# Expert results by indirect transfers through a table in DRAM, in place of matmuls with selection matrices

## The chip, the core and the metric

The kernel runs on one core of a Trainium2 chip. The metric is the device time of one execution in microseconds. Five engines work side by side, each through its own queue in order: PE (TensorE, matmul), DVE (VectorE), ACT (ScalarE), POOL (GpSimd) and SP (SyncE, which here only issues transfers). In this kernel SP issues every transfer and POOL none.

## What is computed

A trunk of two layers works on 272 tokens (16 learned ones and 256 of the input) of 1024 channels: a Griffin recurrent block and a dense SwiGLU, then gated linear attention and a mixture of experts. Each of the four sub-layers ends in `LayerNorm(alpha * x + sublayer(x))`. The change touches the last sub-layer only. Its reference, cut to the core:

```python
logits = hf @ router
top_logit, top_idx = lax.top_k(logits, 2)
top_w = softmax(top_logit)
gates = einsum('nk,nke->ne', top_w, one_hot(top_idx, 8))
for e in range(8):
    y = y + gates[:, e:e+1] * ((silu(hf @ w_gate[e]) * (hf @ w_up[e])) @ w_out[e])
```

Each token goes to two of eight experts. Every expert has 1024 x 7168 and 3584 x 1024 weights in float32, 44 MB, and all of them are read once.

## The kernel before

All large matmuls are done in three passes (`mm3`, L271 to L275): weights and activations are each split into a high and a low part, and low by high, high by low and high by high are summed. The activations (128 x 128) are loaded into the array, and 512 columns of weights stream by. The class `Weights` streams all weights of the program in one fixed order. SP loads units of 128 x 2048 (1 MB) into places of SBUF (`load`, L97), as soon as a place is free; ACT writes the high part of each piece of 1024 columns (`whi`, L127) and DVE the low part (`wlo`, L137), four pieces ahead of the matmuls that take them. When the low part of a unit's last piece is written, its place goes to the next unit. A place can be retired, which hands it to another use.

The experts run one after another, each with room for 128 tokens; a branch at the end repeats the work for more, and it isn't taken when no expert has over 128. An expert has seven blocks (`JM`), so there are 56 blocks `n`. A block is `stage_in` (8 steps `k`, each with three matmuls into the gate bank `pg` and three into the up bank `pu`), four transposes of the product (`stage_tr`, tile `pt`, L1273, done in the next block after three steps), and `stage_out` (24 matmuls into the two output banks `y` of the expert). So a block has 72 matmuls of 512 columns and four transposes. DVE does 12 low parts, one product and one split for it.

Tokens are routed by matmul. `select` (DVE, L931) makes a 0/1 matrix from ranks: tokens by slots of an expert.

- Before a pair of experts, `gather` multiplies the 256 token rows, split in high and low (`x3h`, `x3l`), by the pair's matrices (L940: 32 matmuls of 256 columns for a pair, tile `xg`); ACT and DVE apply gain and bias (L1037, L1035), then split the rows (L268, L269, tile `xe`). Experts 0 and 1 get theirs ahead of the expert loop.
- `slots(e)` transposes the expert's matrix (two transposes, tile `st`, L1229) and fetches the gate of each slot (two matmuls, tile `gs`, L1234).
- After an expert, `evacuate` multiplies its result by the gates and splits it (ACT L1304, DVE L1307), and `combine` multiplies it by the transposed matrix (L1314 and L1315: 8 matmuls of 512 columns an expert, tile `cb`), which DVE adds to the rows `acc` in SBUF (L1317).
- For the last expert, `combine` adds into the banks `total`, into which `add_rows` has put `acc`, split by `split_acc`. Then the final norm follows.

This extra work waits in a list (`Side`). At every second step `k` of `stage_in` one item is taken from it, with up to four saved up. `rows_1` fills the list in expert 0 when the place `xeB` comes free: the rows of expert 1 are split, gates computed, and `acc` is multiplied by the norm's gain, alpha, and added to the bias by `residual` (with `pick` on POOL, L1191, and `sp` on PE, L1197). In the loop at the end of the function the remaining items are put in by block. The framework orders each engine's instructions by priority and by when it reckons them ready.

Fifteen places hold weights when the experts start: nine of the program's own, `late0` to `late3`, `xeC` and `xeB`. `xeB` is retired at block 2 and `xeC` at block 6, and 13 are left.

Of the kernel before, what the change touches and what calls it, by code (L numbers as in the profile page):

```python
# [11 lines left out]
F32 = mybir.dt.float32  # L12
F32R = mybir.dt.float32r
# [172 lines left out]
def trunk_kernel(ctx: ExitStack, tc: tile.TileContext, xT_d, rgp_d, lnT_d, rgin_d, rgg_d, rgout_d,  # L186
# [50 lines left out]
    def bank(name):  # L237
        return ps.tile([P, 512], F32, tag="ps", name=name)
# [678 lines left out]
    pos = small("pos", [P, 2, NE])  # L917
    sels = {}
    late = ctx.enter_context(tc.tile_pool(name="late", bufs=1, reuse_waits="tile"))
    W.widen([(late, "late0"), (late, "late1"), (late, "late2"), (late, "late3"), (late, "xeC")])  # L920
    gb = ctx.enter_context(tc.tile_pool(name="rows", bufs=1, reuse_waits="tile"))
    x3T = [gb.tile([P, 2, NX], F32, tag="xg", name=f"x3T{k2}", bufs=4) for k2 in range(4)]

# [101 lines left out]
    xe, xgs = {}, {}  # L1025

    def rows_of(e):
        pool, tag = ((m2, "xeA"), (m2, "xeB"), (late, "xeC"))[e % 3]
        t = pool.tile([P, 2, KD, P], F32R, tag=tag, name=f"xe{e}", bufs=1)
        xe[e] = (t[:, 0], t[:, 1])  # L1030

    def affine(out, pk, kk, vector):
# [6 lines left out]
    def gathered(pg, e0, k2):  # L1039

        if k2 == 0:
            rows_of(e0)
            rows_of(e0 + 1)
        xg = gb.tile([P, 2, 2, P], F32, tag="xg", name=f"xgs{e0}{k2}", bufs=4)
        for k in range(2):
            affine(xg[:, k], pg[:, k * 256:(k + 1) * 256], 2 * k2 + k, k == 1)
        xgs[e0, k2] = xg

    def first_rows(k2, e):

# [109 lines left out]
    w1 = small("w1", [P, 2, 1])  # L1160
    w2 = small("w2", [P, 2, 1])

    def gate_values():
        pn = bank("count")
        nc.tensor.matmul(pn[:, :NE], ones, mask[:, 0], start=True, stop=False)
        nc.tensor.matmul(pn[:, :NE], ones, mask[:, 1], start=False, stop=True)
        nc.vector.tensor_reduce(cnt, pn[:, :NE], axis=mybir.AxisListType.X, op=ALU.max)
        nc.vector.tensor_copy(cnti, cnt)
        nc.vector.tensor_sub(o2, mask, o1)
        nc.vector.tensor_sub(df, top[:, :, 1:2], top[:, :, 0:1])  # L1170
        nc.scalar.activation(df, df, AF.Exp)
        nc.vector.tensor_scalar_add(w1, df, 1.0)
        nc.vector.reciprocal(w1, w1)
        nc.vector.tensor_mul(w2, df, w1)
        nc.vector.tensor_mul(o1, o1, w1.broadcast_to([P, 2, NE]))
        nc.vector.tensor_mul(o2, o2, w2.broadcast_to([P, 2, NE]))
        nc.vector.tensor_add(gates, o1, o2)

    picks, rows_hl = {}, []

# [22 lines left out]
    def residual(c, s, i):  # L1203

        if i == 0:
            spreads[c, s] = spread(0, c, s)
        a = acc[:, i, s * 512:(s + 1) * 512]
        nc.vector.scalar_tensor_tensor(a, spreads[c, s], ALPHA, a, op0=ALU.mult, op1=ALU.add if c else ALU.mult)


    gslot = m2.tile([P, NE], F32, name="gslot")
    selT = {}
    gus, hts, ys, yes = {}, {}, {}, {}

# [4 lines left out]
    def gather(e0, k2):  # L1219
        pg = bank(f"xg{e0}{k2}")  # L1220
        for i in range(2):
            gather_part(pg, k2, e0, i)
        gathered(pg, e0, k2)

    def slots(e):
# [6 lines left out]
        pg = bank(f"gs{e}")  # L1232
        for i in range(2):
            nc.tensor.matmul(pg[:, :NE], sel_of(e)[:, i].bitcast(F32), gates[:, i], start=(i == 0),  # L1234
                             stop=(i == 1), skip_group_check=True)
        nc.vector.tensor_copy(gslot[:, e:e + 1], pg[:, e:e + 1])

    rows = m2.tile([P, 256], F32, name="rows")
    nc.gpsimd.memset(rows, 0.0)
    for n in range(2):  # L1240
        for p0 in (64 * n, 64 * n + 32):
# [3 lines left out]
    def rows_1():  # L1245
        side.put([lambda: rows_of(1)] + [lambda k2=k2: split_rows(1, k2) for k2 in range(4)]
                 + [spread_split, lambda: behind(chosen, gate_values)]
                 + [lambda c=c: spread_pick(0, c) for c in range(2)]
                 + [lambda c=c, s=s, i=i: residual(c, s, i) for c in range(2) for s in range(2) for i in range(2)])

    def stage_in(n):
        e = n // JM
        xeh, xel = xe[e]
        pg, pu = bank(f"pg{n}"), bank(f"pu{n}")
        for k in range(KD):
            if k == 3 and n > 0:
                stage_tr(n - 1)
            for pp in (pg, pu):
                mm3(pp, (xeh[:, k], xel[:, k]), W.take(512), k == 0, k == KD - 1)
            if k % 2:  # L1260
                side.step()
# [21 lines left out]
    def stage_out(n):  # L1283
# [7 lines left out]
        for b, (q, s) in enumerate(blocks):  # L1291
# [6 lines left out]
            if n == NJ - 1 and b == 6:  # L1298
                finish(0)

    def evacuate(e, s):
        g = gslot[:, e:e + 1]
        yh, yl = [gb.tile([P, 512], F32R, tag="xg", name=f"y{t}{e}{s}", bufs=4) for t in "hl"]
        high = nc.scalar.activation(yh, ys[e][s], AF.Copy, scale=g)  # L1304
        if (e, s) == (NE - 1, 0):
            preload_sqrt(high)
        nc.vector.scalar_tensor_tensor(yl, ys[e][s], g, yh, op0=ALU.mult, op1=ALU.subtract)  # L1307
        yes[e, s] = yh, yl

    def combine(e, i, s):  # L1310
        yh, yl = yes[e, s]
        c = slice(s * 512, (s + 1) * 512)
# [77 lines left out]
    for n in range(NJ + 1):  # L1390
        if n == 1:
            W.after = ()
        if n < NJ:
            stage_in(n)
        if n > 0:
            e, j = (n - 1) // JM, (n - 1) % JM
            if n == NJ:
                side.drain()
            stage_out(n - 1)
            if n == RB:  # L1400
                W.retire("xeB", rows_1)
            if n == JM - 1:
                W.retire("xeC", lambda: None)
            if j == (2 if e % 2 else 4):
                side.put([lambda e=e: slots(e)])
            if j == 2 and e % 2 == 1 and e < NE - 1:
                side.put([lambda e=e: pair(e + 1)])
                side.put([lambda g=g: behind(chosen, lambda: [select(g, i) for i in range(2)]) for g in (e + 1, e + 2)])
                side.put([lambda e=e, k2=k2: gather(e + 1, k2) for k2 in range(4)])
                side.put([lambda g=g, k2=k2: split_rows(g, k2) for g in (e + 1, e + 2) for k2 in range(4)])  # L1410
            if e == NE - 1 and j == 1:
                lng[0] = m2.tile([P, 2, D], F32, tag="xeA", name="lng", bufs=1)
                side.put([lambda c=c: spread_pick(1, c) for c in range(2)] + [lambda: None] * 4)
# [3 lines left out]
            if j == JM - 1:  # L1417
                while e not in selT:
                    side.items.popleft()()
                if e < NE - 1:  # L1420
                    evacuate(e, 0)
                    evacuate(e, 1)
                    side.put([lambda e=e, i=i, s=s: combine(e, i, s) for s in range(2) for i in range(2)])
    evacuate(NE - 1, 1)
    finish(1)

# [160 lines left out]
```

## Time and profile before

| what | value |
|---|---|
| runs | 1553.68, 1556.21, 1557.07 us; median 1556.21 us |
| profiled execution, its own time | 1554.9 us |
| its span (first to last instruction) | 1553.2 us, granted TensorE clock 0.996 |
| busy: PE, DVE, ACT, POOL | 1525.0, 1289.9, 1074.2, 104.2 us |
| moved | 438.61 MB, 282 GB/s over the span |

1.7 us of the execution lie outside the span. Busy time is the union of an engine's instructions. Matmuls are pipelined, so the length of one (some 395 ns) is more than the time to the next (some 230 ns); the price of PE work is therefore read from the distance of equal events in the timeline or from the chain of waits, not from the mean length.

### The profile page before, as it was taken

The page shows a single profiled execution, that of the slowest core. Times are in us where ns is not written, and L with a number is a line of the kernel's source. Part 1 is how long each engine was busy: PE and PEld are TensorE (multiplying, and loading weights), DVE is VectorE, ACT ScalarE, POOL GpSimd, SP SyncE. Part 2 cuts the span into 40 slices and gives each one's busy share as a digit, 9 for nine tenths or more (in the row PEclk, how much of TensorE's full clock was granted, in tenths as well). Part 3 has the DMA queues.
Part 4 walks back from the last instruction along what each step waited for, and adds up shares of the span by engine and source line. Part 5 has one row for each costly group of instructions (what it writes and reads, how often), then busy time and mean ns, then how long its engine had stood idle before and what let it go on. Part 6 is the DMA issues. An engine that isn't in the chain of part 4 may idle for free.

```text
span 1553.2 us, 22491 instructions
## 1 busy us (share of the span) xinstructions
PE 1525.0 (98%) x8495; PEld 1319.0 (85%) x8495; DVE 1289.9 (83%) x1530; ACT 1074.2 (69%) x1402; POOL 104.2 (7%) x139
## 2 busy tenths in 40 slices
PE   9989999999999999999999999999999999999996
PEld 8989999999998888888888888887887888887775
DVE  7699755565876699999999888989888899989887
ACT  6966544444765588877877777777767777767774
POOL 5443000012000000000000000000000000001001
PEclk9999999999999999999999999999999999999998
DMA  9545544455442699889999999999999999999772
GB/s 374 177 142 203 207 173 156 160 174 179 168 169 77 247 370 374 320 319 373 336 347 363 369 328 354 320 374 342 367 365 346 343 352 345 366 366 335 293 247 75
DMA packets 65700, 438.61 MB, mean 282 GB/s; under 512 B 7824, under 2 KB 8112, under 8 KB 17456
## 3 DMA queue, kind: packets, MB, share of 16 engines
q1 hardware_dynamic: 65584, 437.10, 76.3%
q8 instruction: 68, 1.11, 0.3%
q14 instruction: 48, 0.39, 0.1%
HBM read 436.02 MB, written 1.05 MB: 281 GB/s over the span
## 4 chain that ended last, share of the span: by engine, by line
PE 90%; DVE 5%; ACT 2%; issue 1%; POOL 1%; DMA 0%; SPq 0%; DVEq 0%; ACTq 0%; POOLq 0%
PE pg L274 7%; PE y L274 7%; PE pg L273 7%; PE pu L275 7%; PE pu L273 7%; PE pg L275 7%; PE y L275 7%; PE pu L274 7%; PE y L273 7%; PE fg L274 2%; PE fo L273 2%; PE fo L275 2%; PE fo L274 2%; PE fg L275 2%; PE fu L273 2%; PE fg L273 2%
## 5 line engine op out<-in xcount | busy, mean ns | idle before, releaser
L137 DVE TENSOR_TENSOR wlo<-raw,whi 128x1024 fp32r<-128x1024 f32 (+1 forms) x839 | 987.1, 1217 | 145.7 <-ACT whi L127 139.6
L127 ACT CAST whi<-raw 128x1024 fp32r<-128x1024 f32 (+1 forms) x841 | 838.6, 1037 | 176.6 <-PE pu L275 49.2
L274 PE MATMUL pg<-wlo,xe 128*128 128x512 f32 x448 | 180.6, 403 | 0.4 <-DVE wlo L137 0.3
L273 PE MATMUL pg<-whi,xe 128*128 128x512 f32 x448 | 179.6, 401 | 0.7 <-DVE xe L1060 0.7
L273 PE MATMUL pu<-whi,xe 128*128 128x512 f32 x448 | 177.4, 396 | 0.0
L275 PE MATMUL pu<-whi,xe 128*128 128x512 f32 x448 | 177.4, 396 | 0.0
L275 PE MATMUL pg<-whi,xe 128*128 128x512 f32 x448 | 177.0, 395 | 0.0
L274 PE MATMUL y<-wlo,hh 128*128 128x512 f32 x448 | 176.5, 394 | 0.0
L274 PE MATMUL pu<-wlo,xe 128*128 128x512 f32 x448 | 176.3, 394 | 0.0
L275 PE MATMUL y<-whi,hh 128*128 128x512 f32 x448 | 176.1, 393 | 0.0
L273 PE MATMUL y<-whi,hl 128*128 128x512 f32 x448 | 156.4, 391 | 0.0
L274 PEld LDWEIGHTS pg<-wlo,xe 128*128 128x128 f32 x448 | 84.3, 188 | 20.8 <-DVE wlo L137 3.9
L274 PEld LDWEIGHTS y<-wlo,hh 128*128 128x128 f32 x448 | 84.1, 188 | 20.6 <-DVE wlo L137 1.9
L275 PEld LDWEIGHTS pu<-whi,xe 128*128 128x128 f32 x448 | 84.1, 188 | 20.6
L274 PEld LDWEIGHTS pu<-wlo,xe 128*128 128x128 f32 x448 | 84.1, 188 | 20.4
L273 PEld LDWEIGHTS pu<-whi,xe 128*128 128x128 f32 x448 | 84.1, 188 | 20.3
L273 PEld LDWEIGHTS pg<-whi,xe 128*128 128x128 f32 x448 | 84.2, 188 | 18.7 <-DVE xe L1060 0.9
L273 PEld LDWEIGHTS y<-whi,hl 128*128 128x128 f32 x448 | 83.9, 188 | 19.0 <-ACT whi L127 0.2
L275 PEld LDWEIGHTS pg<-whi,xe 128*128 128x128 f32 x448 | 84.2, 188 | 18.1
L275 PEld LDWEIGHTS y<-whi,hh 128*128 128x128 f32 x448 | 84.2, 188 | 17.6
L1265 ACT ACTIVATE hb<-pg 128x512 f32<-128x512 f32 x56 | 33.4, 596 | 93.8 <-PE pg L275 93.8
L1266 DVE TENSOR_TENSOR hb<-hb,pu 128x512 f32<-128x512 f32 x56 | 38.3, 684 | 38.2 <-ACT hb L1265 36.8
(425 smaller groups left out, 2709.3 us busy)
## 6 DMA issues: line engine op xcount, KB each, us to landing
raw<-min SPq DMA_DIRECT2D x216, 1024.0 KB, 7.0
raw<-mout SPq DMA_DIRECT2D x106, 1024.0 KB, 7.3
raw<-fin SPq DMA_DIRECT2D x28, 1024.0 KB, 4.6
raw<-fout SPq DMA_DIRECT2D x16, 896.0 KB, 4.3
raw<-vr SPq DMA_DIRECT2D x8, 1024.0 KB, 4.4
raw<-min SPq DMA_DIRECT2D x16, 512.0 KB, 4.6
raw<-rgin SPq DMA_DIRECT2D x7, 1024.0 KB, 10.7
raw<-rgout SPq DMA_DIRECT2D x8, 704.0 KB, 3.9
```

Source lines behind the costliest of these rows:

```text
L127: self.high[i] = nc.scalar.copy(hi[:, :n], src).ins
L137: low.tensor_sub(lw[:, :n], src, hi[:, :n])
L273: nc.tensor.matmul(out_ap, w[1], xr[0], start=start, stop=False)
L274: nc.tensor.matmul(out_ap, w[0], xr[1], start=False, stop=False)
L275: nc.tensor.matmul(out_ap, w[0], xr[0], start=False, stop=stop)
L1265: behind(W.coming(n, 2), lambda: nc.scalar.activation(hb, pg, AF.Silu))
L1266: nc.vector.tensor_mul(hb, hb, pu)
```

## The change

Experts 0 to 6 no longer combine by matmul, and experts 2 to 7 no longer gather by matmul.

- Two tables in DRAM are added: `x3d` (256 rows) for the token rows after gain and bias, and `yd` (512 rows for results and 128 that nobody reads).
- `slots(e)` fetches four numbers of each slot at once: gate, address of the result, whether it is in use, and the token. It runs for all experts in the first expert, so all the `select`s run there too. `addresses` turns them into row numbers.
- `clear` fills the 512 rows with zeros (POOL, four transfers of 512 KB). `store_x3` writes `acc` to `x3d` (POOL, 1 MB) after `residual`, which no longer applies alpha.
- `fetch(e)` reads the rows of experts 2 to 7 by an indirect transfer (POOL, 512 KB); `turn(e, h)` transposes them (PE, 8 transposes of 128 x 128 an expert) and splits them (ACT and DVE, two of 512 columns each).
- `scatter(e)` multiplies the result of experts 0 to 6 by the gates (ACT and DVE, 512 columns each) and writes it to `yd` by an indirect transfer (POOL, 512 KB).
- In the last expert `fetch_back` reads `yd` (POOL, twice 1 MB), and `add_back` adds both halves to `acc` (DVE, four of 1024 columns), the first with alpha. The subtraction of `split_acc` moves from POOL to DVE. `last_slots` makes the transposed matrix of expert 7, whose results still go by matmul.
- In experts 0 and 7 the list is served at every step instead of every second.
- One place for weights goes (`late3`) to make room for the fetched rows and the results. `xeC` stays with the weights until block 35, where `late1` and `late2` are given up too: 14 places at the start, 13 once `xeB` is retired, and 10 after block 35.

```diff
-    W.widen([(late, "late0"), (late, "late1"), (late, "late2"), (late, "late3"), (late, "xeC")])
+    W.widen([(late, "late0"), (late, "late1"), (late, "late2"), (late, "xeC")])
+    x3d = dram.tile([NX, D], F32, name="x3d")
+    yd = dram.tile([2 * NX + P, D], F32, name="yd")
...
-        pool, tag = ((m2, "xeA"), (m2, "xeB"), (late, "xeC"))[e % 3]
-        t = pool.tile([P, 2, KD, P], F32R, tag=tag, name=f"xe{e}", bufs=1)
+        t = m2.tile([P, 2, KD, P], F32R, tag=("xeA", "xeB")[e % 2], name=f"xe{e}", bufs=1)
...
+        nc.vector.tensor_copy(per_slot[:, :, :, 2], mask)
+        nc.vector.tensor_mul(per_slot[:, :, :, 3], mask, token[:, :, None].broadcast_to([P, 2, NE]))
+        nc.vector.scalar_tensor_tensor(per_slot[:, :, :, 1], o2, float(NX), per_slot[:, :, :, 3], op0=ALU.mult,
+                                       op1=ALU.add)
...
+        nc.vector.tensor_copy(per_slot[:, :, :, 0], gates)
...
-        nc.vector.scalar_tensor_tensor(a, spreads[c, s], ALPHA, a, op0=ALU.mult, op1=ALU.add if c else ALU.mult)
+        (nc.vector.tensor_add if c else nc.vector.tensor_mul)(a, a, spreads[c, s])
...
     def slots(e):
+        pg = bank(f"gs{e}")
+        for i in range(2):
+            nc.tensor.matmul(pg[:, :4], sel_of(e)[:, i].bitcast(F32), per_slot[:, i, e], start=(i == 0),
+                             stop=(i == 1), skip_group_check=True)
+        nc.vector.tensor_copy(slot_of[:, e], pg[:, :4])
...
+    def fetch(e):
+        x3r[e] = late.tile([P, D], F32, tag="x3r", name=f"x3r{e}", bufs=1)
+        nc.gpsimd.indirect_dma_start(x3r[e], None, x3d, at_row(from_u, e))
+
+    def turn(e, h):
+        if h == 0:
+            rows_of(e)
+        pt = bank(f"xt{e}{h}")
+        for k in range(4):
+            nc.tensor.transpose(pt[:, k * P:(k + 1) * P], x3r[e][:, (4 * h + k) * P:(4 * h + k + 1) * P], ident)
+        split(*(t[:, 4 * h:4 * h + 4].rearrange("p k t -> p (k t)") for t in xe[e]), pt)
...
+    def fetch_back():
+        for n in range(2):
+            t = late.tile([P, 2, D], F32, tag=f"late{n + 1}", name=f"back{n}", bufs=1)
+            nc.gpsimd.dma_start(t, yd[n * NX:(n + 1) * NX].rearrange("(i p) d -> p i d", p=P))
+            back.append(t)
...
+                 + [lambda: [slots(e) for e in range(2)]])
+        for e in range(2, NE, 2):
+            side.put([lambda e=e: [pair(e)] + [select(g, i) for g in (e, e + 1) for i in range(2)],
+                      lambda e=e: [slots(g) for g in (e, e + 1)]])
+        side.put([addresses, clear] + [lambda c=c: spread_pick(0, c) for c in range(2)]
+                 + [lambda c=c, s=s, i=i: residual(c, s, i) for c in range(2) for s in range(2) for i in range(2)]
+                 + [store_x3, lambda: None, lambda: fetch(2)])
...
-            if k % 2:
+            if k % 2 or e in (0, NE - 1):
                 side.step()
...
+    def scatter(e):
+        g = slot_of[:, e, 0:1]
+        y = late.tile([P, D], F32, tag="yrow", name=f"yrow{e}", bufs=1)
+        nc.scalar.activation(y[:, :512], ys[e][0], AF.Copy, scale=g)
+        nc.vector.tensor_scalar(y[:, 512:], ys[e][1], g, None, op0=ALU.mult)
+        nc.gpsimd.indirect_dma_start(yd, at_row(dest_u, e), y, None)
...
-        pc = bank(f"cb{e}{i}{s}") if e < NE - 1 else total[i, s]
-        nc.tensor.matmul(pc, selT[e][:, i], yl, start=(e < NE - 1), stop=False)
-        nc.tensor.matmul(pc, selT[e][:, i], yh, start=False, stop=True)
-        if e < NE - 1:
-            nc.vector.tensor_add(rest[0][:, i, c], rest[0][:, i, c], pc)
+        nc.tensor.matmul(total[i, s], selT[e][:, i], yl, start=False, stop=False)
+        nc.tensor.matmul(total[i, s], selT[e][:, i], yh, start=False, stop=True)
...
-        nc.gpsimd.tensor_sub(acc_l[i, s], rest[0][:, i, c], acc_h[0][:, i, c])
+        nc.vector.tensor_sub(acc_l[i, s], rest[0][:, i, c], acc_h[0][:, i, c])
...
-            if n == JM - 1:
-                W.retire("xeC", lambda: None)
-            if j == (2 if e % 2 else 4):
-                side.put([lambda e=e: slots(e)])
-            if j == 2 and e % 2 == 1 and e < NE - 1:
-                side.put([lambda e=e: pair(e + 1)])
-                side.put([lambda g=g: behind(chosen, lambda: [select(g, i) for i in range(2)]) for g in (e + 1, e + 2)])
-                side.put([lambda e=e, k2=k2: gather(e + 1, k2) for k2 in range(4)])
-                side.put([lambda g=g, k2=k2: split_rows(g, k2) for g in (e + 1, e + 2) for k2 in range(4)])
-            if e == NE - 1 and j == 1:
+            if n == 5 * JM:
+                for tag in ("xeC", "late1", "late2"):
+                    W.retire(tag, lambda: None)
+            if j == 3 and 1 <= e < NE - 1:
+                side.put([lambda e=e, h=h: turn(e + 1, h) for h in range(2)])
+                if e < NE - 2:
+                    side.put([lambda e=e: fetch(e + 2)])
+            if e == NE - 1 and j == 0:
...
+                side.put([fetch_back] + [lambda: None] * 8)
+                side.put([lambda k=k, i=i: add_back(k, i) for k in range(2) for i in range(2)])
                 side.put([lambda i=i, s=s: split_acc(i, s) for s in range(2) for i in range(2)])
```

## Rows read from the trace of the kernel before

**Rows 1.** The page: busy engines, and the chain that ended last by engine.
```profile
PE 1525.0 (98%) x8495; PEld 1319.0 (85%) x8495; DVE 1289.9 (83%) x1530; ACT 1074.2 (69%) x1402; POOL 104.2 (7%) x139
...
PE 90%; DVE 5%; ACT 2%; issue 1%; POOL 1%; DMA 0%; SPq 0%; DVEq 0%; ACTq 0%; POOLq 0%
```

**Rows 2.** Who waited for whom, 700 to 1420 us: total us, times, longest.
```profile
PEld pg L274 <- DVE wlo L137: 1.5, 6, 0.3
PEld y L274 <- DVE wlo L137: 1.2, 4, 0.3
```

**Rows 3.** Stretches: length, busy PE, PEld, DVE, ACT, POOL, clock, DMA share, GB/s.
```profile
640.00:1450.00 810.00, 809.98 (x3656) 657.16 (x3655) 736.87 (x741) 608.38 (x695) 5.91 (x4) 1.00 0.95 351
...
1014.90:1032.04 17.14, 17.14 (x78) 13.92 (x77) 15.21 (x16) 12.41 (x15) 0.00 (x0) 1.00 0.98 370
...
641.48:659.09 17.61, 17.61 (x81) 14.38 (x80) 17.61 (x19) 13.49 (x14) 0.00 (x0) 1.00 0.99 364
```

**Rows 4.** Timeline of PE: transposes of the product, one event a block.
```profile
769.52 0.60 PE L1273 MATMUL pt<-ident,hb 128*128 128x128 f32 x4
786.66 0.60 PE L1273 MATMUL pt<-ident,hb 128*128 128x128 f32 x4
805.67 0.60 PE L1273 MATMUL pt<-ident,hb 128*128 128x128 f32 x4
...
874.23 0.60 PE L1273 MATMUL pt<-ident,hb 128*128 128x128 f32 x4
892.03 0.60 PE L1273 MATMUL pt<-ident,hb 128*128 128x128 f32 x4
...
1154.82 0.38 PE L1273 MATMUL pt<-ident,hb 128*128 128x128 f32 x2
1208.40 0.60 PE L1273 MATMUL pt<-ident,hb 128*128 128x128 f32 x4
1264.29 0.60 PE L1273 MATMUL pt<-ident,hb 128*128 128x128 f32 x4
```

**Rows 5.** Chain of waits by time: start, us spent there, what.
```profile
1015.07 0.44 PE pt L1273 x4
...
1015.74 0.23 PE pg L275
```

**Rows 6.** Groups by shape, 660 us to the end: count, busy us, mean ns.
```profile
L269 DVE TENSOR_TENSOR hl<-pt,hh 128x512 fp32r<-128x512 f32 x50 | 34.2, 684 | 4.0 <-ACT hh L268 4.0
...
L1317 DVE TENSOR_TENSOR acc<-acc,cb 128x512 f32<-128x512 f32 x28 | 17.9, 678 | 0.0
L1307 DVE SCALAR_TENSOR_TENSOR yl<-y,gslot,yh 128x512 fp32r<-128x512 f32 x16 | 12.0, 748 | 1.1 <-ACT yh L1304 0.8
...
L269 DVE TENSOR_TENSOR xe<-xgs,xe 128x256 fp32r<-128x256 f32 x24 | 9.5, 417 | 0.0
...
L1035 DVE TENSOR_SCALAR xgs<-xg,par 128x256 f32<-128x256 f32 x12 | 6.5, 541 | 3.1 <-ACT xgs L1037 3.1
...
L931 DVE TENSOR_SCALAR sel<-slot,pos 128x128 fp32r<-128x128 f32 x12 | 2.6, 279 | 0.0
```

**Rows 7.** Timelines of POOL and DVE around the first picks: start, us, instructions.
```profile
624.02 2.33 POOL L1191 TENSOR_TENSOR pick<-ident 128x512 fp32r<-128x512 f32 x2 [92.29 <-DVE xe L269]
...
625.37 2.06 DVE L137 TENSOR_TENSOR wlo<-raw,whi 128x1024 fp32r<-128x1024 f32 x1
...
627.69 1.21 DVE L137 TENSOR_TENSOR wlo<-raw,whi 128x1024 fp32r<-128x1024 f32 x1
```

**Rows 8.** Chain of waits by time, in the last expert.
```profile
1463.30 1.24 DVE wlo L137
```

**Rows 9.** SP's waits (total us, times, longest), and DMA issues (count, size, us to landing).
```profile
SPq L97 <- DVE wlo L137: 1139.9, 390, 16.7
...
raw<-min SPq DMA_DIRECT2D x216, 1024.0 KB, 7.0
```

**Rows 10.** A stretch early in the experts, columns as in rows 3.
```profile
570.00:590.00 20.00, 20.00 (x93) 16.22 (x91) 19.01 (x20) 15.91 (x17) 0.00 (x0) 1.00 1.01 419
```

More of the change, by code (lines that the diff above doesn't have):

```diff
@@ L919, in trunk_kernel @@
     late = ctx.enter_context(tc.tile_pool(name="late", bufs=1, reuse_waits="tile"))
-    W.widen([(late, "late0"), (late, "late1"), (late, "late2"), (late, "late3"), (late, "xeC")])
+    W.widen([(late, "late0"), (late, "late1"), (late, "late2"), (late, "xeC")])
+    dram = ctx.enter_context(tc.tile_pool(name="dram", bufs=1, space=bass.MemoryType.DRAM))
+    x3d = dram.tile([NX, D], F32, name="x3d")
+    yd = dram.tile([2 * NX + P, D], F32, name="yd")
     gb = ctx.enter_context(tc.tile_pool(name="rows", bufs=1, reuse_waits="tile"))
@@ L1037, in affine @@
             nc.scalar.activation(out, pk, AF.Identity, bias=b, scale=g)
[L1039 to L1047, printed above, removed]
     def first_rows(k2, e):
@@ L1161, in trunk_kernel @@
     w2 = small("w2", [P, 2, 1])
+    per_slot = small("per_slot", [P, 2, NE, 4])
+    token = small("token", [P, 2])
+    nc.gpsimd.iota(token, pattern=[[P, 2]], base=0, channel_multiplier=1, allow_small_or_imprecise_dtypes=True)
+    unused = small("unused", [P, 1])
+    nc.gpsimd.iota(unused, pattern=[[0, 1]], base=-2 * NX, channel_multiplier=-1,
+                   allow_small_or_imprecise_dtypes=True)
+    slot_of = small("slot_of", [P, NE, 4])
+    dest = small("dest", [P, NE])
+    dest_u = small("dest_u", [P, NE], U32)
+    from_u = small("from_u", [P, NE], U32)
     def gate_values():
@@ L1207, in residual @@
         a = acc[:, i, s * 512:(s + 1) * 512]
-        nc.vector.scalar_tensor_tensor(a, spreads[c, s], ALPHA, a, op0=ALU.mult, op1=ALU.add if c else ALU.mult)
-    gslot = m2.tile([P, NE], F32, name="gslot")
+        (nc.vector.tensor_add if c else nc.vector.tensor_mul)(a, a, spreads[c, s])
     selT = {}
@@ L1217, in split_rows, with slots, addresses, last_slots @@
         split(xe[e][0][:, 2 * k2:2 * k2 + 2], xe[e][1][:, 2 * k2:2 * k2 + 2], xg[:, :, e % 2])
-    def gather(e0, k2):
-        pg = bank(f"xg{e0}{k2}")
+    def slots(e):
+        pg = bank(f"gs{e}")
         for i in range(2):
-            gather_part(pg, k2, e0, i)
-        gathered(pg, e0, k2)
-    def slots(e):
+            nc.tensor.matmul(pg[:, :4], sel_of(e)[:, i].bitcast(F32), per_slot[:, i, e], start=(i == 0),
+                             stop=(i == 1), skip_group_check=True)
+        nc.vector.tensor_copy(slot_of[:, e], pg[:, :4])
+    placed = []
+    def addresses():
+        nc.vector.scalar_tensor_tensor(dest, slot_of[:, :, 2], unused, slot_of[:, :, 1], op0=ALU.mult, op1=ALU.add)
+        nc.vector.tensor_scalar(dest, dest, unused, None, op0=ALU.subtract)
+        nc.vector.tensor_copy(dest_u, dest)
+        nc.vector.tensor_copy(from_u, slot_of[:, :, 3])
+        placed.append(True)
+    def last_slots():
+        e = NE - 1
         pt = bank(f"st{e}")
@@ L1231, in slots, with at_row, clear, store_x3 @@
         nc.scalar.copy(selT[e], pt[:, :2 * P].rearrange("p (i t) -> p i t", i=2))
[L1232 to L1238, printed above, removed]
+    x3r = {}
+    def at_row(u, e):
+        return bass.IndirectOffsetOnAxis(ap=u[:, e:e + 1], axis=0)
+    def fetch(e):
[8 more added lines that the diff above has]
+        split(*(t[:, 4 * h:4 * h + 4].rearrange("p k t -> p (k t)") for t in xe[e]), pt)
+    def clear():
+        zero = late.tile([P, D], F32, tag="yrow", name="zero", bufs=1)
+        nc.gpsimd.memset(zero, 0.0)
+        for a in range(2 * NX // P):
+            nc.gpsimd.dma_start(yd[a * P:(a + 1) * P], zero)
+    def store_x3():
+        nc.gpsimd.dma_start(x3d.rearrange("(i p) d -> p i d", p=P), acc)
+    back = []
+    def fetch_back():
[3 more added lines that the diff above has]
+            back.append(t)
+    def add_back(n, i):
+        a = acc[:, i]
+        if n == 0:
+            nc.vector.scalar_tensor_tensor(a, a, ALPHA, back[0][:, i], op0=ALU.mult, op1=ALU.add)
+        else:
+            nc.vector.tensor_add(a, a, back[1][:, i])
+    rows = late.tile([P, D], F32, tag="yrow", name="rows", bufs=1)[:, :256]
     nc.gpsimd.memset(rows, 0.0)
@@ L1247, in rows_1 @@
                  + [spread_split, lambda: behind(chosen, gate_values)]
-                 + [lambda c=c: spread_pick(0, c) for c in range(2)]
-                 + [lambda c=c, s=s, i=i: residual(c, s, i) for c in range(2) for s in range(2) for i in range(2)])
+                 + [lambda: [slots(e) for e in range(2)]])
[5 more added lines that the diff above has]
+                 + [store_x3, lambda: None, lambda: fetch(2)])
     def stage_in(n):
@@ L1299, in stage_out @@
                 finish(0)
+    def scatter(e):
[4 more added lines that the diff above has]
+        nc.gpsimd.indirect_dma_start(yd, at_row(dest_u, e), y, None)
     def evacuate(e, s):
-        g = gslot[:, e:e + 1]
+        g = slot_of[:, e, 0:1]
         yh, yl = [gb.tile([P, 512], F32R, tag="xg", name=f"y{t}{e}{s}", bufs=4) for t in "hl"]
@@ L1311, in combine @@
         yh, yl = yes[e, s]
-        c = slice(s * 512, (s + 1) * 512)
-        pc = bank(f"cb{e}{i}{s}") if e < NE - 1 else total[i, s]
-        nc.tensor.matmul(pc, selT[e][:, i], yl, start=(e < NE - 1), stop=False)
-        nc.tensor.matmul(pc, selT[e][:, i], yh, start=False, stop=True)
-        if e < NE - 1:
-            nc.vector.tensor_add(rest[0][:, i, c], rest[0][:, i, c], pc)
+        nc.tensor.matmul(total[i, s], selT[e][:, i], yl, start=False, stop=False)
+        nc.tensor.matmul(total[i, s], selT[e][:, i], yh, start=False, stop=True)
     outv = out.rearrange("(a p) d -> p a d", p=P)
@@ L1401, in trunk_kernel @@
                 W.retire("xeB", rows_1)
-            if n == JM - 1:
-                W.retire("xeC", lambda: None)
-            if j == (2 if e % 2 else 4):
-                side.put([lambda e=e: slots(e)])
-            if j == 2 and e % 2 == 1 and e < NE - 1:
-                side.put([lambda e=e: pair(e + 1)])
-                side.put([lambda g=g: behind(chosen, lambda: [select(g, i) for i in range(2)]) for g in (e + 1, e + 2)])
-                side.put([lambda e=e, k2=k2: gather(e + 1, k2) for k2 in range(4)])
-                side.put([lambda g=g, k2=k2: split_rows(g, k2) for g in (e + 1, e + 2) for k2 in range(4)])
-            if e == NE - 1 and j == 1:
+            if n == 5 * JM:
[6 more added lines that the diff above has]
+            if e == NE - 1 and j == 0:
                 lng[0] = m2.tile([P, 2, D], F32, tag="xeA", name="lng", bufs=1)
-                side.put([lambda c=c: spread_pick(1, c) for c in range(2)] + [lambda: None] * 4)
+                side.put([last_slots] + [lambda c=c: spread_pick(1, c) for c in range(2)] + [lambda: None] * 4)
                 side.put([lambda c=c, s=s: nc.scalar.copy(lng[0][:, c, s * 512:(s + 1) * 512], spread(1, c, s))
                           for c in range(2) for s in range(2)])
+                side.put([fetch_back] + [lambda: None] * 8)
+                side.put([lambda k=k, i=i: add_back(k, i) for k in range(2) for i in range(2)])
                 side.put([lambda i=i, s=s: split_acc(i, s) for s in range(2) for i in range(2)])
-            if j == JM - 1:
-                while e not in selT:
+            if j == JM - 1 and e < NE - 1:
+                while not placed:
                     side.items.popleft()()
[L1420 to L1423, printed above, removed]
+                scatter(e)
     evacuate(NE - 1, 1)
```

## The prediction

> **What bounds the kernel now.** I read the page first: PE is busy for 98% of the span and carries 90% of the chain that ended last [rows 1]. A busy PE could still be one that waits, so the second view is who waited for whom between 700 and 1420 us, the middle of the experts: nothing holds up the array for more than 0.3 us at a time, and the two longest entries come to 2.7 us in 720 [rows 2]. The third view is the timeline of PE. The four transposes of a block's product are a mark that comes once a block. Where nothing is added the marks are 17.14 us apart (769.52 to 786.66), and that is 72 matmuls at 0.23 and four transposes for 0.44 [rows 4, 5]. So a block is as long as its PE work, and whatever PE does besides is added to the time in full. That is the main premise of the sum.
>
> Two others are near. DVE needs 15.21 us of a plain block of 17.14, and in expert 0, where it has extra work, 17.61 of 17.61 [rows 3]. The DMA engines are busy for 95% of the 810 us between 640 and 1450, at 351 GB/s [rows 3]; but the queue that issues the weights spends 1139.9 us waiting for a low part to be written, which frees a place [rows 9], so the transfers follow the consumption and don't set it. How much faster they can go is in rows 10: 419 GB/s over 20 us.
>
> **PE work that goes.** Combine: in the block from 786.66 to 805.67 it makes 19.01 out of 17.14, so 1.87 us; in the three blocks from 1154.82 to 1208.40 it makes 53.58 out of 51.42, so 2.16 [rows 4]. Eight matmuls at 0.23 alone would be 1.84 [rows 5]. I take 2.0, seven times: 14.0 (12.9 to 15.1). Gather: the three blocks from 1208.40 to 1264.29 take 55.89, 4.47 too long; one `slots` is in there, whose price is 17.80 less 17.14, 0.66 (874.23 to 892.03) [rows 4]. That leaves 3.81 a pair, 11.4 for three. Of `slots` two transposes go for seven experts, at a quarter of 0.44 each [rows 5]: 7 x 0.22, 1.5. Together 26.9.
>
> **PE work that comes.** `turn` is four transposes of the same size as those of a block, twelve times 0.44 [rows 5]: 5.3. The gate matmuls of `slots` stay, with four columns in place of eight; they only move to expert 0 (0.66 less 0.22, so 0.44 an expert). Net: 26.9 less 5.3 is 21.6.
>
> **DVE.** Over all experts it loses 28 additions at 0.678, 14 splits of results at 0.748, 24 splits of rows at 0.417 and 12 affine halves at 0.541: 46 us [rows 6]. It gets 12 splits of 512 columns (0.684 [rows 6]) for `turn`, seven scalings at about 0.7, four `add_back` of 1024 columns (a low part of that size is 1.21 [rows 7]) and four subtractions of `split_acc` (0.684): some 21 us. So experts 1 to 6 are lighter than before, and two places are heavier.
>
> Expert 0: all twelve later `select`s at 0.279 come here (3.3), one scaling (0.7), and some 16 small instructions, at most 0.279 each (4.5); four additions and two splits of expert 0's result leave (4.2) [rows 6]. That is up to 4.3 more for DVE where PE gets only 3.1 for seven gate fetches, less the combine of 2.0. DVE is full there, so up to 3.2 us could come out as waiting PE. But with DVE full before, these blocks were no longer than their PE work (641.48 to 659.09 is 17.61, a plain block and four matmuls of 256 columns), since the low parts are four pieces ahead, 24 matmuls or 5.5 us. I charge 1 (0 to 3.2).
>
> Expert 7: `add_back` 4.8, `split_acc` 2.7 and a scaling 0.7 come, additions and splits of expert 6 for 4.2 go, all in a few blocks: 4.0 more on DVE, with 2.0 less on PE, and slack of 1.93 a block. Before, PE already waited for a low part here once at 1463 [rows 8]. I charge 1 (0 to 6; it could gain 1.2 if that wait goes).
>
> **POOL** issues 20 transfers, of which the trace of before has none. In its queue, `pick` stands behind `clear`, and PE's `sp` waits for `pick`; POOL is busy for only 5.91 us of 810 [rows 3], so it runs ahead of its place, and this costs nothing unless an issue takes many us. What an issue does to DVE is unknown. The nearest row is `pick`: while two of them ran (2.33 us), a low part took 2.06 in place of 1.21 [rows 7], so 0.85. Bounds: nothing, or 0.85 for each of 20. Thirteen of them fall where DVE has 1.93 a block to spare; seven (four of `clear`, `store_x3`, the first fetch, the first scatter) fall in or beside expert 0, up to 6 us. I take nothing, as an issue moves no tile of that size. The Trainium skill (SBUF — State Buffer, Who interferes with whom) says that a DVE instruction with two SBUF inputs and a GpSimd instruction that reads SBUF block one another. By that rule, on which the trace agrees for `pick` (2.06 against 1.21), each issue that reads its row numbers would cost something, and the sum would move towards the first rival.
>
> **Transfers.** The change adds 12.1 MB: 2.1 for `clear`, 1.05 to store the rows, six fetches and seven scatters of 0.52, 2.1 back. In the stretch from 640 to 1450, 284 MB passed [rows 3]; 20 us less and 12 more make 375 GB/s, under the 419 of rows 10. A block takes six units, so one each 2.86 us; 13 places are 37 us ahead, less 7.0 to land [rows 9], 30; with ten places it is still 21. The wait that leaves with a free place on SP is thus covered, and fewer places cost nothing as long as landing stays well below 20 us. Waits that come: PE's `turn` on a fetch that was issued an expert earlier (three blocks, 51 us, for the first one), DVE's `add_back` on `fetch_back`, which POOL can issue as soon as expert 6 is scattered, some three blocks ahead. Two times 1 MB at half of 419 are 10 us. Hidden.
>
> **Sum.** 21.6 less 1 and 1 is 19.6. The profiled execution took 1554.9 us, so 1535.3; it is 1.3 below the median of the runs, hence 1536.6. The terms' own bounds: 24 at best (15.1 + 11.4 + 1.5 - 5.3 + 1.2), that is 1532.
>
> **Rivals.**
> *DVE becomes the bound in experts 0 and 7.* For it: 17.61 of 17.61 [rows 3], and POOL's issues on top. Against it: the lead of 5.5 us, and that the slack behind expert 0 is larger than before. Full price 3.2 + 6 + 6, 15 us in place of the 2 charged: 1549 to 1550. The same time would come if one chain on POOL (`clear`, scatter, store, fetch) were so slow that PE stood at the first `turn` for some 13 us; it has 51 us.
>
> *The DMA engines are at their limit (slower).* For it: a busy share of 0.95. If 351 GB/s is what they give among these matmuls, 296 MB need 843 us where PE needs 790. The lead of ten places covers 21 of the 53, and 32 are lost against 20 gained: some 12 above the median, 1568. It decides from about 356 GB/s down (296 MB in 790 + 20 + 21 us). Against it: 419 GB/s with PE and DVE at full work [rows 10], and a queue that waits for places [rows 9]. The Trainium skill (DMA: Bandwidth & Descriptors, Where 436 GB/s comes from) gives about 358 GB/s as what HBM yields one core. By that, an estimate of 16 us would be lost and the time would be near 1552; the trace has 419, so the measurement decides.
>
> *The work goes, but the time doesn't*, since something else takes PE's place all through (ACT, or DVE at every block): that needs DVE at 17.1 a block, and it is at 15.2 and gets lighter. About 1555.
>
> **How the numbers follow.** Forecast with its terms' bounds, 1532 to 1545: 0.77. DVE or POOL in experts 0 and 7, 1545 to 1552: 0.11. No change: 0.03. DMA limit, slower: 0.09. About 0.2% (3 us) is what a measurement can tell from no change, so faster is 0.77 + 0.11, 0.88; same 0.03; slower 0.09. The range goes from 1531 to 1551, which takes in the first rival; the DMA limit stays outside.
>
> **What would show it.** `cb` and `xg` gone after the first expert's rows; blocks of experts 1 to 6 at 17.14 except one each with `turn` (0.88 more); blocks of expert 0 longer by their `gs` only. Wrong: PE idle before `pg` or `y` released by a low part in blocks 4 to 8 or 50 to 54 (first rival); raw landing times well over 7 us, and ACT's high parts waiting for DMA (second); PE waiting at `xt` for a transfer.

## The result, and the profile after

| | before | after |
|---|---|---|
| median of 4 runs each, same chip | 1555.89 us | 1538.64 us (1536.07 to 1539.52) |
| ratio after to before, 95% interval | | 0.9885 [0.9872, 0.9898] |
| span of the profiled execution | 1553.2 us | 1536.8 us |
| granted TensorE clock, mean | 0.996 | 0.991 |

The change gains 17.2 us by the medians and 16.4 by the profiled spans; 19.6 were forecast. The time is near the forecast, but it is the sum of a gain and of losses that the forecast doesn't have.

The page of the kernel after, busy engines, one DMA queue (packets, MB, share of the engines), the chain that ended last by engine, and one DMA issue:

```profile
PE 1496.2 (97%) x8377; PEld 1305.5 (85%) x8377; DVE 1267.0 (82%) x1487; ACT 1057.8 (69%) x1364; POOL 125.6 (8%) x158
...
q0 software_dynamic: 3264, 12.06, 2.0%
...
PE 88%; DVE 6%; ACT 2%; issue 2%; DMA 1%; POOL 1%; SPq 0%; DVEq 0%; POOLq 0%; ACTq 0%
...
raw<-min SPq DMA_DIRECT2D x216, 1024.0 KB, 7.1
```

PE is busy for 28.8 us less than in [rows 1] while the span is only 16.4 shorter: 12.4 us of new idle time, and PE has 88% of the chain in place of 90%. The queue q0 holds POOL's transfers, 12.06 MB. A weight unit still lands in 7.1 us (7.0 in [rows 9]).

The kernel after in stretches (length, busy PE, PEld, DVE, ACT, POOL, clock, DMA share, GB/s): the middle of the experts, one plain block, one block in expert 0, one in expert 7, and 4 us within each of the last two:

```profile
640.00:1390.00 750.00, 750.00 (x3402) 616.81 (x3401) 676.97 (x649) 568.83 (x629) 19.14 (x13) 1.00 0.97 372
...
1021.98:1038.92 16.94, 16.94 (x77) 13.91 (x76) 15.00 (x15) 11.52 (x15) 0.00 (x0) 1.00 0.99 371
...
618.28:643.45 25.17, 22.65 (x97) 18.60 (x96) 23.14 (x35) 14.50 (x18) 10.21 (x9) 0.86 0.86 304
...
1396.89:1426.40 29.51, 20.03 (x78) 15.88 (x76) 18.98 (x19) 14.95 (x17) 2.97 (x3) 0.83 0.82 314
...
632.00:636.00 4.00, 3.59 (x13) 3.23 (x14) 3.40 (x10) 0.42 (x1) 2.61 (x5) 0.58 0.97 381
1414.00:1418.00 4.00, 0.00 (x0) 0.00 (x0) 1.98 (x2) 0.00 (x0) 0.00 (x0) 0.53 0.60 245
```

In the middle PE has no idle time at all. Two blocks at its edges are 25.17 and 29.51 us long. In both PE stands, and while it stands or right behind it the granted clock falls: 0.58 and 0.53 in those 4 us, about the lower of TensorE's two levels (1.2 and 2.4 GHz).

Who waited for whom in the kernel after (total us, times, longest):

```profile
DVE acc L1293 <- DMA back<-yd: 10.2, 1, 10.2
...
PE y L274 <- DVE wlo L137: 9.5, 1, 9.5
...
POOL back L1287 <- DMA yd<-yrow,dest_u: 7.6, 1, 7.6
...
PE gs L1230 <- DVE sel L934: 2.5, 1, 2.5
```

The two of PE are all of its waits over 2 us in the experts. The timeline of PE in the kernel after, the marks of [rows 4], and the six-matmul pattern of a block (start, us, instruction):

```profile
734.98 0.60 PE L1337 MATMUL pt<-ident,hb 128*128 128x128 f32 x4
750.53 1.03 PE L1268 MATMUL xt<-ident,x3r 128*128 128x128 f32 x8
752.79 0.60 PE L1337 MATMUL pt<-ident,hb 128*128 128x128 f32 x4
786.67 0.60 PE L1337 MATMUL pt<-ident,hb 128*128 128x128 f32 x4
803.61 0.60 PE L1337 MATMUL pt<-ident,hb 128*128 128x128 f32 x4
...
860.37 0.39 PE L273 MATMUL pg<-whi,xe 128*128 128x512 f32 x1
...
861.75 0.62 PE L273 MATMUL y<-whi,hl 128*128 128x512 f32 x2
863.12 0.62 PE L273 MATMUL y<-whi,hl 128*128 128x512 f32 x2
```

A plain block is 16.94 us (786.67 to 803.61), where [rows 4] had 17.14 for the same instructions. A block with `turn` is 17.81, 0.87 more (other such blocks up to 0.93 more). And six matmuls take 1.38 us at `pg` and 1.37 at `y`. The kernel before, the same view:

```profile
860.32 0.40 PE L273 MATMUL pg<-whi,xe 128*128 128x512 f32 x1
...
861.72 0.40 PE L273 MATMUL pg<-whi,xe 128*128 128x512 f32 x1
...
864.53 0.40 PE L273 MATMUL y<-whi,hl 128*128 128x512 f32 x1
...
867.97 0.39 PE L273 MATMUL y<-whi,hl 128*128 128x512 f32 x1
```

There, six matmuls with `xe` take 1.40 us (0.2333 each), and the 15 with `hh` and `hl` from 864.53 to 867.97 take 0.2293 each. 48 matmuls of a block by 0.004 are 0.19 us: the whole difference between the blocks, and for 56 blocks 11 us. So three questions stood open: why `xe` matmuls come faster, what holds PE in expert 0, and what holds it in expert 7.

### The profile page after: what moved, and what is told of

Read it like the earlier page. It is cut to its first block, busy times and chain, and to the rows that moved or that the text cites. A ratio compares the mean times of both kernels' runs of the same rounds, so it can differ in the third digit from the quotient of the medians.

```text
span 1536.8 us, 22261 instructions
## 1 busy us (share of the span) xinstructions
PE 1496.2 (97%) x8377; PEld 1305.5 (85%) x8377; DVE 1267.0 (82%) x1487; ACT 1057.8 (69%) x1364; POOL 125.6 (8%) x158
## 3 DMA queue, kind: packets, MB, share of 16 engines
q0 software_dynamic: 3264, 12.06, 2.0%
## 4 chain that ended last, share of the span: by engine, by line
PE 88%; DVE 6%; ACT 2%; issue 2%; DMA 1%; POOL 1%; SPq 0%; DVEq 0%; POOLq 0%; ACTq 0%
PE y L274 7%; PE y L275 7%; PE y L273 7%; PE pg L273 7%; PE pg L274 6%; PE pu L273 6%; PE pg L275 6%; PE pu L275 6%; PE pu L274 6%; DVE wlo L137 2%; PE fg L274 2%; PE fo L273 2%; PE fo L275 2%; PE fu L273 2%; PE fg L275 2%
## 5 line engine op out<-in xcount | busy, mean ns | idle before, releaser
L273 PE MATMUL y<-whi,hl 128*128 128x512 f32 x448 | 152.5, 396 | 0.0
L273 PEld LDWEIGHTS y<-whi,hl 128*128 128x128 f32 x448 | 85.1, 190 | 18.4
```

Of the source, the lines that this page charges most:

```text
L273: nc.tensor.matmul(out_ap, w[1], xr[0], start=start, stop=False)
```

## The experiments

Each is timed against the kernel before on the same chip (its median there was 1556.37 us for the first four, 1556.74 for the others). The kernel after wasn't timed again beside them: "less than after" compares with the 1538.64 us of the first table, taken where the kernel before had 1555.89.

**The start address.** The allocation of the built programs, which is no part of a profile, differs: before, the `xe` tiles start 32 bytes past a multiple of 64 (204320, for one) and `hh` at one (223808); after, both start at multiples of 64 (204864 and 223296), since the change drops and adds small tiles ahead of them. Theory: that alone sets the pitch. Rival: it comes with the work that left the blocks. The first test puts unused tiles of 32 bytes into the kernel before:

```diff
+    small("pad32", [P, 8])
     cnt = small("cnt", [P, 1])
...
     gslot = m2.tile([P, NE], F32, name="gslot")
+    m2.tile([P, 8], F32, name="pad32b")
```

> The kernel before, with two unused tiles of 32 bytes a partition, so that the stationary tiles of the expert matmuls (xe, and hh as before) start at a multiple of 64 bytes, as in the changed kernel. Theory 'start address': matmuls on xe come every 229 ns in place of 232 to 234, a plain block takes 16.94 us in place of 17.14, and 55 of them give 11 us: about 1545. Rival 'the work around them' (less PE and DVE work beside the matmuls made them faster): nothing changes, 17.14 and 1556.

Measured: 1545.23 us (1541.73 to 1546.03), ratio 0.9926 [0.991, 0.9943], a gain of 11.1 us with the same instructions in the same order. The timeline of PE in this kernel, two marks of plain blocks:

```profile
1007.71 0.60 PE L1275 MATMUL pt<-ident,hb 128*128 128x128 f32 x4
1024.60 0.60 PE L1275 MATMUL pt<-ident,hb 128*128 128x128 f32 x4
```

16.89 us from one to the next. Of the 0.05 us to the 16.94 of the kernel after, 0.03 lie in the 24 matmuls with `hh` and `hl` (5.46 us from 1018.68, 5.49 from 861.75 there). These two tiles start at a multiple of 128 in this program and 64 past one in the kernel after; whether that is the reason wasn't tested. The second test does the opposite to the kernel after, moving all later tiles by 32 bytes:

```diff
+    small("pad32", [P, 8])
     cnt = small("cnt", [P, 1])
```

> The changed kernel with one unused tile of 32 bytes, which moves xe and hh to 32 bytes past a multiple of 64. Theory 'start address': all 72 matmuls of a block, not 48 as before the change, come some 4 ns later, so a plain block takes 17.2 to 17.25 us in place of 16.94, and the time is 1554 to 1556. Rival 'the work around them': 16.94 and 1538.6.

Measured: 1553.63 us (1549.54 to 1559.15), ratio 0.9976 [0.9965, 0.9988]. The same view:

```profile
859.62 0.40 PE L274 MATMUL y<-wlo,hh 128*128 128x512 f32 x1
860.32 0.39 PE L274 MATMUL y<-wlo,hh 128*128 128x512 f32 x1
...
862.61 0.39 PE L273 MATMUL pg<-whi,xe 128*128 128x512 f32 x1
864.01 0.39 PE L273 MATMUL pg<-whi,xe 128*128 128x512 f32 x1
...
1017.98 0.60 PE L1338 MATMUL pt<-ident,hb 128*128 128x128 f32 x4
1035.23 0.60 PE L1338 MATMUL pt<-ident,hb 128*128 128x128 f32 x4
```

A block is 17.25 us, and now the matmuls with `hh` are slow too (three in 0.70 us; six with `xe` in 1.40). 15.0 us are lost by 32 bytes that nothing reads. The address theory holds and the rival falls. That it is the address of the tile loaded into the array, and not of the weights that stream by, follows from two things. The weights' tiles `whi` and `wlo` start at the same multiples of 64 in all four programs, and in the kernel before, where `pg` and `y` matmuls stream from them alike, only those with `xe` are slow. No test moved one tile alone, and no offset but 32 of 64 was tried.

**The wait in expert 7.** The timeline of DVE in the kernel after (in brackets the idle time before an instruction, and what ended it):

```profile
1403.44 2.35 DVE L137 TENSOR_TENSOR wlo<-raw,whi 128x1024 fp32r<-128x1024 f32 x2
1416.02 1.23 DVE L1293 SCALAR_TENSOR_TENSOR acc<-acc,back 128x1024 f32<-128x1024 f32 x1 [10.24 <-DMA back<-yd]
```

The first `add_back` stands in DVE's queue at 1405.8, when its rows are not there: POOL issues `fetch_back` at 1407.98, after waiting 7.6 us for expert 6's scatter to land, and DVE waits for it until 1416.02. Behind it stand the low parts that PE needs, and PE stands for 9.5 us. Theory: it is this place in the queue. Rival: DVE has too much work in this expert, and the time comes back elsewhere. The test ties `add_back` to the product of the newest block, so that it can't be queued ahead of it:

```diff
-        nc.vector.tensor_mul(hb, hb, pu)
+        product.append(nc.vector.tensor_mul(hb, hb, pu).ins)
...
-                side.put([lambda k=k, i=i: add_back(k, i) for k in range(2) for i in range(2)])
+                side.put([lambda k=k, i=i: behind(product[-1:], lambda: add_back(k, i)) for k in range(2) for i in range(2)])
```

> The changed kernel with add_back queued on DVE behind the latest product of a block, about three blocks after its place now. Theory: the wait of 10.2 us on DVE for the returned rows goes, with it PE's 9.5 us and the slow clock after it, together 12.6 us in the block of 29.5: about 1526. Rival 'the returned 2 MB hold up the weights themselves, or the order only shifts the wait to another place in the last expert': 1534 or more.

Measured: 1528.2 us (1527.11 to 1529.06), ratio 0.9813 [0.9796, 0.9829], 10.4 less than after. The block is back at its PE work and the rest of the expert in blocks (columns as above):

```profile
1397.30:1414.24 16.94, 16.94 (x78) 13.91 (x76) 15.75 (x16) 12.87 (x15) 2.98 (x3) 1.00 0.98 392
1414.24:1432.93 18.69, 18.56 (x87) 14.96 (x86) 14.69 (x15) 16.32 (x21) 0.00 (x0) 1.00 1.02 420
1432.93:1450.15 17.22, 17.20 (x77) 13.83 (x76) 16.05 (x16) 12.92 (x15) 0.00 (x0) 1.00 0.80 314
1450.15:1467.82 17.67, 16.70 (x74) 13.03 (x73) 17.67 (x18) 13.54 (x18) 0.00 (x0) 1.00 0.54 174
1467.82:1486.19 18.37, 18.12 (x82) 14.70 (x81) 18.37 (x19) 13.91 (x16) 0.00 (x0) 1.00 0.91 320
```

12.6 us are won in the first (29.51 to 16.94), and 2.8 are lost in the four behind it (71.95 against 69.15 in the kernel after), where DVE is now busy for 17.67 of 17.67 and 18.37 of 18.37. So the place in the queue cost 12.6, and some 3 us of that come back behind it. That DVE's excess in this expert is their cause is likely, as its rows are full, but not shown: PE is idle for only 1.4 us in these four rows.

**The wait in expert 0.** The timelines of POOL and DVE in the kernel after:

```profile
618.52 3.06 POOL L1199 TENSOR_TENSOR pick<-ident 128x512 fp32r<-128x512 f32 x2 [92.12 <-PE y L275]
622.02 1.89 POOL L1199 TENSOR_TENSOR pick<-ident 128x512 fp32r<-128x512 f32 x1 [0.43 <-DVE xe L269]
624.33 1.89 POOL L1199 TENSOR_TENSOR pick<-ident 128x512 fp32r<-128x512 f32 x1 [0.43 <-DVE xe L269]
...
632.52 2.42 POOL L1276 DMA_DIRECT2D yd<-zero  x4 [0.33 <-POOL zero L1274]
```

```profile
618.63 2.06 DVE L137 TENSOR_TENSOR wlo<-raw,whi 128x1024 fp32r<-128x1024 f32 x1
620.62 1.25 DVE L269 TENSOR_TENSOR xe<-xgs,xe 128x256 fp32r<-128x256 f32 x1
622.93 1.26 DVE L269 TENSOR_TENSOR xe<-xgs,xe 128x256 fp32r<-128x256 f32 x1
624.11 4.33 DVE L137 TENSOR_TENSOR wlo<-raw,whi 128x1024 fp32r<-128x1024 f32 x3
631.36 1.35 DVE L934 TENSOR_SCALAR sel<-slot,pos 128x128 fp32r<-128x128 f32 x4
```

Four `pick`s run in this block, the two for the last expert among them, ahead of `clear`; each costs one DVE instruction with two SBUF inputs some 0.84 (2.06 for 1.21, 1.25 for 0.42, 4.33 for three of 1.16). So the `sel` matrices come 3.4 us late, PE stands at `gs` for 2.5, and then works at the low clock. Theory: the picks. Rival: the many small steps from `gs` to `slot_of` and back. The test leaves DVE its work and holds the picks back behind POOL's transfers:

```diff
-        nc.gpsimd.tensor_add(picks[n, c], high, low)
+        behind(issued[-1:], lambda: nc.gpsimd.tensor_add(picks[n, c], high, low))
...
-            nc.gpsimd.dma_start(yd[a * P:(a + 1) * P], zero)
+            issued.append(nc.gpsimd.dma_start(yd[a * P:(a + 1) * P], zero).ins)
...
-        nc.gpsimd.indirect_dma_start(yd, at_row(dest_u, e), y, None)
+        issued.append(nc.gpsimd.indirect_dma_start(yd, at_row(dest_u, e), y, None).ins)
```

> The changed kernel with the picks on POOL queued behind clear (the first two) and behind the latest scatter (the other two), so that none of the four runs while DVE splits the rows of expert 1. Theory 'POOL's picks hold up DVE': four DVE instructions took 0.85 us too long each; without that the selects come 3.4 us earlier, the wait of PE at the gate fetch and most of the slow clock after it go: 4 to 6 us, 1533 to 1535. Rival 'the single selection tile, which PE and DVE hand to and fro': the block of 25.2 us stays within 1 us, 1538.

Measured: 1534.42 us (1531.57 to 1535.31), ratio 0.9857 [0.9841, 0.9873], 4.2 less than after (6.9 by the profiled spans, of which 6.1 lie between the first and the last mark of the experts). The same block and 4 us within it:

```profile
617.41:636.64 19.23, 19.23 (x98) 16.16 (x97) 18.77 (x32) 14.54 (x18) 6.36 (x7) 1.00 0.95 344
...
632.00:636.00 4.00, 4.00 (x19) 3.26 (x19) 4.00 (x7) 3.04 (x4) 1.69 (x2) 1.00 1.04 376
```

19.23 in place of 25.17, PE without a wait, the clock at 1.00 in place of 0.58, though the chain of small steps is unchanged. The picks it was.

**Both edits together**, to see whether they add up.

> The changed kernel with both edits: add_back queued behind the latest product, and the picks behind clear and the latest scatter. If the two waits are independent, both savings add: 10.4 and 4.2 off 1538.6 is 1524; the block with the gate fetches at 19.2 us, the one of 29.5 at 16.9. If one only took over from the other (the second is hidden behind the first), 1528.

Measured: 1526.84 us (1525.28 to 1527.21), ratio 0.9813 [0.9799, 0.9826]. In its profile both long blocks are gone (19.22 and 17.39 us) and the span is 1523.5 us, but the runs place it only 1.4 below the first edit alone, with an equal ratio. The two profiles put the picks higher: the block in expert 0 takes 23.58 us with the first edit alone, 4.4 more than with both, and the time between the first and the last mark differs by 3.9. So runs and profiles don't agree on what the picks are worth once the other wait is gone.

**Spreading `add_back`.** If the 2.8 us in expert 7 come from four `add_back` too close together, three steps between them should win them back:

```diff
-                side.put([fetch_back] + [lambda: None] * 8)
-                side.put([lambda k=k, i=i: behind(product[-1:], lambda: add_back(k, i)) for k in range(2) for i in range(2)])
+                side.put([fetch_back] + [lambda: None] * 2)
+                side.put([f for k in range(2) for i in range(2)
+                          for f in (lambda k=k, i=i: behind(product[-1:], lambda: add_back(k, i)), lambda: None, lambda: None)])
```

> As both, with the four add_back set three steps apart in the list instead of one after another. Theory: in the last expert DVE is over-full for two blocks (blocks 50 to 53 were some 3 us longer than their PE work in the run with add_back later); spread out, 1 to 2.5 us of that go: 1521.5 to 1523. Rival: that excess comes from the splits of acc and the norm rows on ACT, and stays: 1524.

Measured: 1528.99 us (1523.06 to 1530.63), ratio 0.9819 [0.9801, 0.9837]: nothing won. The four blocks take 72.5 us together, 71.9 without this edit. The excess stays and moves between blocks; what it comes from and what would remove it is still open.

**The DMA engines' limit.** To the version with both edits, 42 copies of 1 MB from DRAM to DRAM were added, one a block, each issued by SP right behind a weight unit:

```diff
             self.nc.sync.dma_start(t[:, :n], ap)
+            if self.copies and i in self.copies:
+                with self.tc.issue_after(ins):
+                    self.nc.sync.dma_start(self.junk.tile([P, n], F32, name=f"junk{i}"), ap)
```

> As both, with 42 further transfers of 1 MB (DRAM to DRAM, issued by SP behind the weights, one a block in experts 1 to 6), that nobody reads. A block then moves 7.65 MB. Theory: the DMA engines' limit is near the 419 GB/s that the stretch from 570 to 590 us showed; a block needs 18.25 us in place of 16.94, the lead of 30 us is used up after some 23 blocks and the rest lose 1.3 us each: 1545 to 1555. Rival 'limit at 351 GB/s': 21.8 us a block, over 1650. Rival 'the limit is not near': 1524.

Measured in one run: 1547.07 us. The middle of the experts (columns as above), and, in a second view, the weight issues (count, size, us to landing):

```profile
640.00:1390.00 750.00, 739.75 (x3314) 605.23 (x3313) 659.75 (x637) 549.80 (x614) 16.30 (x13) 0.99 1.01 421
```

```profile
raw<-min SPq DMA_DIRECT2D x216, 1024.0 KB, 14.0
```

The engines gave 421 GB/s over 750 us, PE being busy for 739.75 of them. Their busy share is 1.01, where 0.97 went with 372 GB/s in the kernel after, so a share near 1 didn't mean that no more could pass. Landing went from 7.1 to 14.0, and still no engine waited for a weight unit for more than 0.2 us. What was lost lies elsewhere, in the six blocks with `turn`. Who waited for whom there:

```profile
ACT xe L272 <- PE xt L1273: 27.7, 12, 2.5
...
PE pg L277 <- ACT whi L131: 7.1, 6, 1.2
```

ACT's high parts now stand behind splits of `xe` that wait for `turn`: another order of the instructions, not a lack of transfers. (The chain on this run's page has 3% DMA, from three places where a part of a unit happens to land as ACT goes on from such a split; ACT starts its next high part some 0.5 us after the split there, as at the places without a landing.) So the time, which lies where a limit of the engines was to put it, doesn't speak for that limit. A limit at 351 GB/s is refuted; where it lies above 421 wasn't measured.

**Ten places.** Retiring the three places at the start of expert 1 instead of after block 35, in the version with both edits:

```diff
-            if n == 5 * JM:
+            if n == JM:
                 for tag in ("xeC", "late1", "late2"):
```

> As both, with three places for weights given up after the first expert instead of after the fifth: ten places through experts 1 to 7. Theory: a lead of 28 us less some 7 to land is enough, no change within 0.2%, 1524. Rival 'fewer places starve the matmuls as soon as fetches and scatters share the engines': ACT waits for weights, 3 us or more longer.

Measured: 1525.4 us (1524.33 to 1525.45), ratio 0.98 [0.9785, 0.9815]; the middle of the experts:

```profile
640.00:1390.00 750.00, 750.00 (x3403) 616.82 (x3402) 678.25 (x652) 569.03 (x630) 20.34 (x13) 1.00 0.97 374
```

PE has no idle time with ten places either. This is the lowest time measured, 31.3 us below the kernel before and 13.2 below the change as it was made.

## Why the prediction was near, and where it was wrong

**PE's own work: right.** `cb` and the later `xg` are gone and `turn` came at 0.87 to 0.93 in six blocks, some 5.5 us for the 5.3 predicted. That makes the net of 21.6 a 21.4. At equal offsets from 64, and with the two long waits gone, the sum can be compared: 1545.2 (the kernel before, moved) to 1526.8 (both edits) is 18.4, and to 1525.4 it is 19.8; the forecast was 19.6 with its two charges.

**"Blocks of experts 1 to 6 at 17.14": wrong.** The sum took the pitch of a matmul as fixed ("72 matmuls at 0.23"). It is 0.2293 or 0.2333 by the start address of a tile, and the change moved that address: 56 times 0.20 us, 11.2, against 11.1 by the medians of the test that moves the address alone. The two pitches stood in the trace of before, side by side in each block; rounded to 0.23 they can't be seen.

**Expert 0, "I charge 1 (0 to 3.2)": wrong in cause and size.** 5.9 us were lost (25.17 less 19.23). DVE's work as such costs nothing: without the early picks the block is as long as its PE work. The step that failed is in the part on POOL, "in its queue, `pick` stands behind `clear`": the picks ran first, and not two but four of them, apparently because the framework reckoned POOL and the picks' inputs free by then. Their price of 0.85 was known [rows 7], the place was assumed. The Trainium skill (SBUF — State Buffer, Who interferes with whom) says that a DVE instruction with two SBUF inputs contends with a GpSimd instruction that reads SBUF. For the four picks the trace agrees, with some 0.84 each.

**POOL's issues, "I take nothing": right.** What the prediction drew from the rule just named for issues that read row numbers, a price for each, is not there. A scatter is issued from 1040.35 to 1041.92 in the kernel after, and the four low parts around it take 4.63 us, as do four without one; low parts that run beside the other issues take 1.21 to 1.23 us each, too. The timelines of POOL and DVE:

```profile
1040.35 1.57 POOL L1371 DMA_INDIRECT yd<-yrow,dest_u  x1 [47.75 <-ACT whi L127]
```

```profile
1034.27 4.63 DVE L137 TENSOR_TENSOR wlo<-raw,whi 128x1024 fp32r<-128x1024 f32 x4 [0.25 <-ACT whi L127]
...
1039.85 4.63 DVE L137 TENSOR_TENSOR wlo<-raw,whi 128x1024 fp32r<-128x1024 f32 x4 [0.29 <-ACT whi L127]
```

**Expert 7, "`add_back` on `fetch_back` ... Hidden": the largest miss.** The prediction asked when POOL could issue the fetch, "some three blocks ahead", and how long it takes. Both count from the end of expert 6, and so does the place that `add_back` got in DVE's queue, ahead of the data. It named a wait on DVE without asking what stands behind it: low parts, and so PE. 12.6 us, of which 9.5 are PE's wait and the rest mostly the low clock behind it. The charge of "1 (0 to 6)" was for DVE's extra work; that is some 3 us at most and came to light only when this wait was gone. The wait of [rows 8] for a low part went as the prediction allowed (1.2).

**The balance:** 21.4 and 11.2 and 1.2 gained, 5.9 and 12.6 lost, is 15.3 gained; the profiled spans have 16.4. An error of 11.2 in favour and one of 16.5 against (18.5 lost where 2 were charged) cancel but for 5.3. The forecast's "faster" held for its main reason, its time by luck.

**The rivals.** *DVE the bound in experts 0 and 7*, with a full price of 15 us: these are the places where 18.5 us were lost, but through an order on two queues and not through too much work. *The DMA engines at their limit*: refuted, with 372 GB/s and PE at 750.00 of 750.00. The 12.1 MB came as counted. The Trainium skill (DMA: Bandwidth & Descriptors, Where 436 GB/s comes from) gives about 358 GB/s as the limit of HBM for one core, half of what two cores share. In the run with copies this kernel's one core moved 421 for 750 us, so here the measurement decides. *No change*: in the middle of the experts every us of PE work removed was gained.

## What to carry to other kernels

Where a kernel is bound by matmuls, read their pitch to the nanosecond per operand; before an edit is judged by its time, a version of the old kernel with the new tile addresses shows what the addresses alone do, and a 32-byte tile that nothing uses can be worth 11 us. An instruction that waits for a transfer costs what stands behind it in its queue, so look up where the scheduler puts it and tie it to a later instruction if that is too early. Work that was harmless in its old place has to be placed anew in the mind, and then in the code, when its queue or its inputs come free earlier.

## What the runs showed that was not expected

- Matmuls of 512 columns come every 229 ns, or every 233 ns when the tile in the array starts 32 bytes past a multiple of 64 (in these kernels): 16.89 to 16.94 us a block, 17.14 with two thirds of the matmuls on such a tile, 17.22 to 17.25 with all.
- A wait of PE costs more than itself. After 9.5 us of waiting the block was 12.6 longer, after 2.5 us it was 5.9 longer, with granted clocks of 0.53 and 0.58 in the stretches beside the waits. The price isn't fixed: the same wait of 2.5 us made the block 4.4 longer in the profile of the run with `add_back` later, where the clock over the block was 0.93 and not 0.86.
- One core's DMA engines moved 421 GB/s for 750 us while PE, DVE and ACT worked, and a landing time twice as long (14.0 us) hurt no engine.
